# Low parts of weights made by an accumulating DMA instead of a subtraction on VectorE

## The chip, the core and the metric

The kernel runs on one core of a Trainium2 chip. The core has five engines that run their own instruction queues in order and meet at semaphores: TensorE (PE, with its weight loads shown as PEld), VectorE (DVE), ScalarE (ACT), GpSimd (POOL) and SyncE (SP, which issues the kernel's DMAs). Sixteen DMA engines move the data. The metric is the time of one execution on the device in microseconds, as a median of several runs; lower is better.

## What is computed

One layer of a hybrid backbone, for 128 context tokens and 512 latent tokens of width 1024, which the kernel holds side by side as 640 columns:

```python
h = rmsnorm(x, norm1) * (1 + sc1) + sh1
p = h @ w_in
qkv, z, ab, glu, gates = jnp.split(p, SPLITS, axis=-1)
qkv = jax.nn.silu(dwconv_seq(qkv, conv_qkv))
...
o, s_fin = bidir_delta(q, k, v, g, beta, s0)      # 8 heads, chunked delta rule, both directions
y_a = (rmsnorm(o, norm_o) * silu(z)) @ w_a_out
y_b = silu(layernorm(dwconv(glu branch), ln_g, ln_b)) @ w_b_out
x = x + g1 * ((ga * y_a + gb * y_b) @ w_o)
gu = (rmsnorm(x, norm2) * (1 + sc2) + sh2) @ w_gu
x = x + g2 * ((silu(gu[..., :FF_DIM]) * gu[..., FF_DIM:]) @ w_down)
```

The weights and the activations are float32. The context's delta states are an output beside the two token blocks.

## The kernel before

**A product of two float32 matrices is made of three products.** Each operand is split into a high part (the value rounded to the type float32r, `wh`, `hh`) and a low part (what the rounding left, `wl`, `hl`). A projection adds `wh*hh`, `wh*hl` and `wl*hh` in PSUM. The helper `split` (lines 106 to 108) makes both parts: ACT writes the high part (line 107), and DVE or POOL subtracts it from the raw value (line 108).

**Weights.** `load_w` (line 117) brings a block of 128 columns of a weight matrix, 1024 rows in 8 tiles of 128, so 128 partitions x 1024 float32, 512 KB: SP issues the load into `wr` (line 121), then `split` writes `wh` and `wl`. A `wl` lies in the same bytes as its `wr`; there are 4 such slots (`NWR`) and 2 buffers for `wh` (`NWH`). During most of the input projection every second slot carries raw weights of the modulation matrix `w_ada` (line 458), so a projection's slot comes back every second projection. `low["eng"]` chooses who subtracts: DVE until the delta rule and the branches beside it have ended, POOL after that.

**Projections.** `proj` (line 131) goes over the `nk` tiles of a weight block (8, or 4 for the two branch outputs) and for each over the three products and two column halves of 256 and 384; the matmul is line 143. A full projection is 48 matmuls. 56 such projections make up `w_in`: 24 for q, k and v, 8 for z, 16 for the gates, 8 for the convolution branch. `w_a_out` (first half of its rows) and `w_b_out` add 8 each of 4 tiles before the switch of `low["eng"]`.

**Beside them** run the steps of the delta rule for four pairs of heads: short convolutions and a substitution on DVE (lines 478, 593 to 611), small matmuls on PE, evacuations of PSUM on ACT, masks, powers and casts on POOL (lines 516, 584, 598, 607, 623, 650). Generators yield estimated costs, and a scheduler that works on an estimated timeline sets each engine's order when the program is built, so a queue's order is fixed and an instruction that waits holds what stands behind it. After the switch come the output projection and the FFN.

Of the kernel before, what the change touches and what calls it, by code (L numbers as in the profile page):

```python
# [9 lines left out]
F32 = mybir.dt.float32  # L10
# [4 lines left out]
AF = mybir.ActivationFunctionType  # L15
ALU = mybir.AluOpType
# [3 lines left out]
P = 128  # L20
# [36 lines left out]
def hybrid_step(ctx, tc, I, O):  # L57
    nc = tc.nc
    es = ctx.enter_context
    V, S_, G, PE = nc.vector, nc.scalar, nc.gpsimd, nc.tensor  # L60
# [39 lines left out]
    def g3(ap, a):  # L100
        return ap.rearrange("p (a b) -> p a b", a=a)
# [4 lines left out]
    def split(hi, lo, x, lo_eng=None):  # L106
        S_.activation(hi, x, AF.Identity)  # L107
        return (lo_eng or V).tensor_tensor(out=lo, in0=x, in1=hi.bitcast(F32), op=ALU.subtract)  # L108
# [3 lines left out]
                          mybir.DependencyInfo(mybir.DependencyClass.NoSync, mybir.DependencyReason.DATA),  # L112
                          reason="order")

    low = {"eng": V}

    def load_w(src, lo_eng=None, after=None, wh=None):
        a, b = src.shape[1], src.shape[2]
        n = a * b
        wr, wl = next(w_next)  # L120
        ld = nc.sync.dma_start(out=g3(wr[:, :n], a), in_=src)
        if after is not None:
            order(ld, after)
        wh = T_("wh", "wh", F32R) if wh is None else wh
        split(wh[:, :n], wl[:, :n], wr[:, :n], lo_eng or low["eng"])
        return g3(wh[:, :n], a), g3(wl[:, :n], a)

    def cols_of(w, c0, n=P):
# [2 lines left out]
    def proj(w, xh, xl, nk, pp=None, hfs=(0, 1), cut=HALVES, tiled=False):  # L131
        pp = pp or mm_pair()
        wh, wl = w
        for kt in range(nk):
            for j, (a, b) in enumerate(((wh, xh), (wh, xl), (wl, xh))):
                for hf in hfs:
                    c = cut[hf]
                    out, x = pp[hf][:, :c.stop - c.start], b[kt // 4]
                    if tiled:
                        out, x = g3(out, (c.stop - c.start) // P), x[:, c.start // P:c.stop // P, kt % 4, :]  # L140
                    else:
                        x = x[:, kt % 4, c]
                    PE.matmul(out, a[:, kt, :], x,  # L143
                              start=(kt == 0 and j == 0), stop=(kt == nk - 1 and j == 2))
        return pp

    def halves(pp, ap, cut=HALVES):
# [21 lines left out]
    for k, (nm, n) in enumerate((("c_ctx", 8), ("c", 8), ("norm1", 8), ("norm2", 8))):  # L169
        src = I[nm] if nm == "c_ctx" else I[nm][0]  # L170
# [89 lines left out]
    for pr in range(4):  # L260
# [7 lines left out]
        for kk in range(NK):  # L268
            for g in range(4):
                j, k = g // 2, g % 2  # L270
                PE.matmul(pa[32 * g:32 * g + 32, :P], sc[:, kk, 14:46], ws[j][:, kk, 128 * k:128 * k + 128],
                          start=(kk == 0), stop=(kk == NK - 1), tile_position=(0, 32 * g))
# [4 lines left out]
        for k in range(2):  # L277
            kt = 2 * pr + k
# [1009 lines left out]
```

## Time and profile before

| what | us |
|---|---|
| median of 3 runs (1337.16 to 1340.9) | 1338.35 |
| profiled execution, whole | 1341.02 |
| its span, first to last instruction | 1339.2 |
| PE busy | 1278.0 (95%) |
| DVE busy | 845.0 (63%) |
| ACT busy | 505.2 (38%) |
| POOL busy | 299.7 (22%) |

A profile shows for every engine when each instruction ran, which line and tiles it belongs to, and what ended the idle time before it. Busy shares over the whole span hide that the stages differ: DVE is at nine tenths or more in many slices of the first 800 us and at a quarter after. Matmuls overlap in the pipeline, so PE can be called busy and still not run at full pace; how fast a projection goes is better read from the starts of its matmuls.

### The profile page before, as it was taken

What the parts mean: (1) busy time and instruction counts of PE and PEld (TensorE: products, weight loads), DVE (VectorE), ACT (ScalarE), POOL (GpSimd) and SP (SyncE); (2) the same over time, 40 slices, a digit from 0 to 9 for tenths busy, and PEclk for the clock granted to TensorE, in tenths of its full rate; (3) what the DMA queues carried; (4) which work ended last, traced back from release to release, by engine and by line L of the source; (5) the groups of instructions that cost most, each with busy time, mean ns of one, the idle gap of its engine ahead of it and who ended that gap; (6) DMA issues with size and microseconds to landing.
All of it is one profiled execution on the core that took longest, in us unless ns stands there. A gap on an engine that the chain in (4) does not pass through costs nothing.

```text
span 1339.2 us, 23242 instructions
## 1 busy us (share of the span) xinstructions
PE 1278.0 (95%) x9180; PEld 1203.7 (90%) x9180; DVE 845.0 (63%) x1663; ACT 505.2 (38%) x1080; POOL 299.7 (22%) x306
## 2 busy tenths in 40 slices
PE   4998998997999999999998999999999999999997
PEld 4998997997998999999988998899988999889996
DVE  5788996989667899998687774621224212243136
ACT  3426646254354554525354323422221222112223
POOL 2103312220110312211010036433300333003304
PEclk8998999999999999999999999999999999999999
DMA  9523353343343453324456882122222222222222
GB/s 290 153 64 97 113 167 123 112 139 99 109 122 102 142 144 101 105 78 128 142 188 202 286 281 87 52 76 79 79 74 70 78 80 75 68 79 79 79 68 91
DMA packets 180333, 157.31 MB, mean 117 GB/s; under 512 B 9072, under 2 KB 151809, under 8 KB 180225
## 3 DMA queue, kind: packets, MB, share of 16 engines
q1 hardware_dynamic: 180225, 155.83, 37.6%
q8 instruction: 72, 1.18, 0.4%
q14 instruction: 36, 0.29, 0.1%
HBM read 131.80 MB, written 24.00 MB: 116 GB/s over the span
## 4 chain that ended last, share of the span: by engine, by line
PE 57%; DVE 8%; DMA 3%; issue 2%; ACT 2%; POOL 1%; SPq 0%; POOLq 0%; DVEq 0%; ACTq 0%
PE mm L143 36%; PE sm L1108 9%; PE mm L1108 4%; PE sm L143 1%; DVE wl L108 1%; PE sm L729 1%; DVE uacc L843 1%; PE sm L753 1%; PE sm L656 1%; DVE uacc L840 1%; PE sm L1153 1%; PE sm L716 1%; PE sm L709 1%; PE sm L739 1%; DMA wr<-in_w_in 1%
## 5 line engine op out<-in xcount | busy, mean ns | idle before, releaser
L107 ACT ACTIVATE wh<-wr 128x1024 fp32r<-128x1024 f32 (+1 forms) x154 | 152.6, 992 | 477.2 <-PE mm L143 186.1
L143 PE MATMUL mm<-hh,wh 128*128 128x256 f32 (+1 forms) x896 | 217.6, 318 | 0.9 <-ACT wh L107 0.9
L143 PE MATMUL mm<-hl,wh 128*128 128x256 f32 (+1 forms) x896 | 215.4, 314 | 0.0
L108 POOL TENSOR_TENSOR wl<-wr,wh 128x1024 fp32r<-128x1024 f32 (+1 forms) x59 | 133.2, 2259 | 356.7 <-ACT wh L107 337.2
L143 PE MATMUL mm<-hh,wl 128*128 128x256 f32 (+1 forms) x896 | 212.5, 314 | 0.0
L108 DVE TENSOR_TENSOR wl<-wr,wh 128x1024 fp32r<-128x1024 f32 (+1 forms) x95 | 109.7, 1155 | 105.7 <-ACT wh L107 94.4
L143 PEld LDWEIGHTS mm<-hh,wh 128*128 128x128 f32 x896 | 161.5, 190 | 6.8 <-issue 4.6
L143 PEld LDWEIGHTS mm<-hl,wh 128*128 128x128 f32 x896 | 164.5, 189 | 0.0
L143 PEld LDWEIGHTS mm<-hh,wl 128*128 128x128 f32 x896 | 162.7, 189 | 0.3 <-issue 0.2
L143 PE MATMUL mm<-h2h,wh 128*128 128x256 f32 (+1 forms) x672 | 155.7, 309 | 0.0
L143 PE MATMUL mm<-h2l,wh 128*128 128x256 f32 (+1 forms) x672 | 154.9, 308 | 0.0
L143 PE MATMUL mm<-h2h,wl 128*128 128x256 f32 (+1 forms) x672 | 154.6, 307 | 0.0
L1254 DVE TENSOR_TENSOR ft<-ft,mm 128x256 f32<-128x256 f32 (+1 forms) x42 | 18.6, 481 | 189.9 <-PE mm L143 189.8
L143 PEld LDWEIGHTS mm<-h2l,wh 128*128 128x128 f32 x672 | 123.1, 188 | 0.0
L143 PEld LDWEIGHTS mm<-h2h,wl 128*128 128x128 f32 x672 | 122.7, 188 | 0.0
L143 PEld LDWEIGHTS mm<-h2h,wh 128*128 128x128 f32 x672 | 122.0, 188 | 0.2
L478 DVE SCALAR_TENSOR_TENSOR acc<-ci,colA,acc 128x642 f32<-128x642 f32 x96 | 85.8, 894 | 7.6 <-ACT acc L476 7.1
L1108 PE MATMUL sm<-wh,fl 128*128 128x512 f32 x152 | 60.0, 395 | 0.0
L1108 PE MATMUL sm<-wh,fh 128*128 128x512 f32 x152 | 59.8, 393 | 0.0
L1108 PE MATMUL sm<-wl,fh 128*128 128x512 f32 x152 | 59.6, 392 | 0.0
L108 DVE TENSOR_TENSOR fl<-ft,fh 128x640 fp32r<-128x640 f32 x22 | 46.5, 2112 | 16.5 <-ACT fh L107 16.5
L604 DVE TENSOR_TENSOR stmp<-M,X 128x30 f32<-128x30 f32 (+14 forms) x120 | 44.6, 372 | 2.6 <-POOL X L598 1.0
(347 smaller groups left out, 2446.8 us busy)
## 6 DMA issues: line engine op xcount, KB each, us to landing
wr<-in_w_in SPq DMA_DIRECT2D x56, 512.0 KB
wr<-in_w_gu SPq DMA_DIRECT2D x44, 512.0 KB
wr<-in_w_ada SPq DMA_DIRECT2D x32, 512.0 KB
wr<-in_w_down SPq DMA_DIRECT2D x22, 512.0 KB
wada<-in_w_ada SPq DMA_DIRECT2D x8, 1024.0 KB
atd<-et SPq DMA_DIRECT2D x40, 128.0 KB
aux<-atd SPq DMA_DIRECT2D x40, 128.0 KB
tgd<-tgt SPq DMA_DIRECT2D x16, 320.0 KB
```

The source lines that it names most:

```text
L107: S_.activation(hi, x, AF.Identity)
L108: return (lo_eng or V).tensor_tensor(out=lo, in0=x, in1=hi.bitcast(F32), op=ALU.subtract)
L143: PE.matmul(out, a[:, kt, :], x, start=(kt == 0 and j == 0), stop=(kt == nk - 1 and j == 2))
L478: V.scalar_tensor_tensor(out=acc[:, :n], in0=ci[:, k:k + n], scalar=vA[:, k, ct:ct + 1], in1=acc[:, :n], op0=ALU.mult, op1=ALU.add)
L604: V.tensor_tensor(out=t, in0=bc(M[:, j + 1:, j:j + 1], [P, n, j]), in1=bc(X[:, j:j + 1, 0:j], [P, n, j]), op=ALU.mult)
L656: PE.matmul(pt[:, j, :], lhs[j], rhs[j], start=True, stop=True)
L709: PE.matmul(pr[:, d, j, :], TT[j].kT[:, ck[d], :], S[:, d, j, :], start=True, stop=True)
L716: PE.matmul(pq[:, d, j, :], TT[j].q2[:, OFFC[ck[d]]:OFFC[ck[d]] + P], S[:, d, j, :], start=True, stop=True)
L729: PE.matmul(pv[:, d, j, :], Y1[:, d, j, ck[d], :], rhs, start=True, stop=True)
L739: PE.matmul(pS[:, d, j, :], TT[j].ktok[:, ck[d], :], vw[:, d, j, :], start=True, stop=True)
L1108: PE.matmul(acc[i], a[kt // 4][:, kt % 4, c], b[:, k2, :], start=(kt == 0 and j == 0), stop=(kt == nk - 1 and j == 2))
L1254: V.tensor_tensor(out=d, in0=d, in1=s, op=ALU.mult)
```

## The change

While `low["eng"]` is `None`, which it is from the start until the delta rule and the branches end, `load_w` no longer subtracts. ACT writes `wh` from the raw weights as before, then ACT writes minus `wh` into `wl`, over the raw weights, and then POOL issues a DMA that reads the same weights from memory a second time and adds them onto `wl`. After the switch `split` works on POOL as before; calls that name an engine keep it. The second edit is in `proj`, for all projections: all products with `wh` come first, over all weight tiles, and all products with `wl` come after them.

```diff
-    low = {"eng": V}
+    low = {"eng": None}
...
-        split(wh[:, :n], wl[:, :n], wr[:, :n], lo_eng or low["eng"])
+        if lo_eng is None and low["eng"] is None:
+
+            S_.activation(wh[:, :n], wr[:, :n], AF.Identity)
+            S_.activation(wl[:, :n], wh[:, :n].bitcast(F32), AF.Identity, scale=-1.0)
+            G.dma_start(out=g3(wl[:, :n], a), in_=src, accum_op=ALU.add)
+        else:
+            split(wh[:, :n], wl[:, :n], wr[:, :n], lo_eng or low["eng"])
...
-        for kt in range(nk):
-            for j, (a, b) in enumerate(((wh, xh), (wh, xl), (wl, xh))):
-                for hf in hfs:
-                    c = cut[hf]
...
+        three = ((wh, xh), (wh, xl), (wl, xh))
+
+        for kt, j in [(kt, j) for kt in range(nk) for j in range(2)] + [(kt, 2) for kt in range(nk)]:
+            a, b = three[j]
+            for hf in hfs:
+                c = cut[hf]
```

The built program has 72 accumulating DMAs (56 of `w_in`, 8 of `w_a_out`, 8 of `w_b_out`), 72 more activations on ACT and 72 fewer subtractions on DVE. The changed code is 8 lines longer, so a line of before stands 8 higher there.

On PE, in the first projections of heads, the three products alternated with each weight tile. Before, at the fourth and fifth tile of one projection (the suffixes 132 and 133 are the two halves of the activations' rows):

```order
L143 MATMUL mm<-hh_132,wh 128x256
L143 MATMUL mm<-hh_132,wh 128x384
L143 MATMUL mm<-hl_134,wh 128x256
L143 MATMUL mm<-hl_134,wh 128x384
L143 MATMUL mm<-hh_132,wl_60 128x256
L143 MATMUL mm<-hh_132,wl_60 128x384
L143 MATMUL mm<-hh_133,wh 128x256
L143 MATMUL mm<-hh_133,wh 128x384
```

And in the change, at the end of the high weights of such a projection:

```order
L151 MATMUL mm<-hh_133,wh 128x256
L151 MATMUL mm<-hh_133,wh 128x384
L151 MATMUL mm<-hl_135,wh 128x256
L151 MATMUL mm<-hl_135,wh 128x384
L151 MATMUL mm<-hh_132,wl_58 128x256
L151 MATMUL mm<-hh_132,wl_58 128x384
```

The first matmul that reads `wl` is now the 33rd of 48; it was the 5th.

On POOL, around the end of the first pair's substitution (X, and its casts into XB) and the start of the second pair's masks, before:

```order
L584 AFFINE_SELECT Bt<-Bt 128x640 x2
L607 MEMSET X 128x32
L623 CAST XB<-T_1579 32x10x32 x4
L623 CAST XB<-T_1580 32x10x32 x4
L589 MEMSET Cc 128x384
L598 AFFINE_SELECT X<-M 128x1024
L650 TENSOR_TENSOR L_671<-Bt,off_102 128x512
```

And in the change (wl_56 and wl_60 are the low parts in two of the four slots):

```order
L129 DMA wl_56<-in_w_in 128x8x128
L592 AFFINE_SELECT Bt<-Bt 128x640 x2
L615 MEMSET X 128x32
L631 CAST XB<-T_1587 32x10x32 x4
L631 CAST XB<-T_1588 32x10x32 x4
L597 MEMSET Cc 128x384
L129 DMA wl_60<-in_w_in 128x8x128
L129 DMA wl_56<-in_w_in 128x8x128
L606 AFFINE_SELECT X<-M 128x1024
L129 DMA wl_60<-in_w_in 128x8x128
```

The DMAs stand between steps that wait for DVE: the masks, the memset of X and the casts all do. Of the 72 DMAs, 33 have at least one such step (a mask, a power, a memset of X, a cast or an off-diagonal product) between themselves and the DMA ahead.

## Rows read from the trace of the kernel before

**Rows 1.** Busy time of each engine by stage; PEclk is the granted clock.
```profile
core 0: us, PE busy (x) PEld busy (x) DVE busy (x) ACT busy (x) POOL busy (x), PEclk, DMA share, GB/s
0.00:100.00 100.00, 81.30 (x718) 77.61 (x719) 74.29 (x174) 35.49 (x67) 14.66 (x50) 0.93 0.56 170
100.00:500.00 400.00, 376.21 (x3145) 350.93 (x3143) 330.39 (x689) 207.59 (x550) 84.02 (x133) 0.98 0.40 123
500.00:650.00 150.00, 148.40 (x1161) 145.09 (x1160) 142.28 (x336) 65.65 (x121) 28.41 (x28) 1.00 0.36 105
650.00:800.00 150.00, 140.49 (x1045) 137.36 (x1044) 108.89 (x227) 56.10 (x132) 18.05 (x15) 0.98 0.70 226
800.00:1339.00 539.00, 531.62 (x3121) 492.73 (x3119) 189.13 (x239) 140.32 (x210) 154.60 (x80) 0.99 0.25 77
```

**Rows 2.** PE's longest waits, 100 to 500 us: total, times, longest.
```profile
PE sm L656 <- ACT XA L621: 4.6, 2, 2.3
PE sm L489 <- DVE K L523: 4.3, 1, 4.3
PE sm L739 <- DVE vw L735: 4.2, 2, 2.5
PE sm L709 <- ACT Sn L742: 2.1, 1, 2.1
```

**Rows 3.** Splits on DVE, 100 to 500 us: busy, mean ns | idle before.
```profile
L108 DVE TENSOR_TENSOR wl<-wr,wh 128x1024 fp32r<-128x1024 f32 x32 | 40.2, 1256 | 18.6 <-ACT wh L107 18.3
```

**Rows 4.** DVE and ACT, lines 108 and 107, 0 to 770 us.
```profile
L108 DVE TENSOR_TENSOR wl<-wr,wh 128x1024 fp32r<-128x1024 f32 (+1 forms) x72 | 81.5, 1133 | 32.2 <-ACT wh L107 31.7
...
L107 ACT ACTIVATE wh<-wr 128x1024 fp32r<-128x1024 f32 (+1 forms) x73 | 70.0, 959 | 130.9 <-PE mm L143 74.6 <-DMA wr<-in_w_in 50.9 <-DMA wr<-in_w_b_out 3.9
```

**Rows 5.** Two weight loads, issue and first reader: start, us, engine.
```profile
121.91 0.42 SPq L121 DMA_DIRECT2D wr<-in_w_in  x1
...
126.12 1.06 ACT L107 ACTIVATE wh<-wr 128x1024 fp32r<-128x1024 f32 x1 [0.68 <-DMA wr<-in_w_in]
...
17.32 3.61 SPq L121 DMA_DIRECT2D wr<-in_w_in  x1
...
28.64 1.06 ACT L107 ACTIVATE wh<-wr 128x1024 fp32r<-128x1024 f32 x1 [11.75 <-DMA wr<-in_w_in]
```

**Rows 6.** A piece of the chain that ended last: start, us, what.
```profile
353.83 7.57 DMA wr<-in_w_in
```

**Rows 7.** A tight projection: ACT timeline; PE matmuls, first and last start.
```profile
455.99 1.06 ACT L107 ACTIVATE wh<-wr 128x1024 fp32r<-128x1024 f32 x1 [0.19 <-DMA wr<-in_w_in]
...
L143 PE MATMUL mm<-hh,wh x16: 278/336/384, 458.6 to 464.9; 128*128 128x256 f32 x8, 128*128 128x384 f32 x8
...
L143 PE MATMUL mm<-hh,wl x16: 279/336/367, 459.2 to 466.6; 128*128 128x256 f32 x8, 128*128 128x384 f32 x8
```

**Rows 8.** A loose projection, the same three views.
```profile
524.90 1.06 ACT L107 ACTIVATE wh<-wr 128x1024 fp32r<-128x1024 f32 x1 [5.33 <-PE mm L143]
...
L143 PE MATMUL mm<-hh,wh x16: 278/336/365, 533.1 to 542.5; 128*128 128x256 f32 x8, 128*128 128x384 f32 x8
...
L143 PE MATMUL mm<-hh,wl x18: 279/331/364, 532.8 to 544.0; 128*128 128x256 f32 x9, 128*128 128x384 f32 x9
```

**Rows 9.** SP timeline: two successive loads into one weight slot.
```profile
439.94 0.37 SPq L121 DMA_DIRECT2D wr<-in_w_in  x1
...
458.11 0.38 SPq L121 DMA_DIRECT2D wr<-in_w_in  x1
```

**Rows 10.** POOL's waits for DVE, 100 to 500 us: total, times, longest.
```profile
POOL rn L516 <- DVE rn L515: 88.5, 14, 12.9
POOL Bt L584 <- DVE Bt L578: 63.2, 6, 15.9
...
POOL X L607 <- DVE X L606: 20.4, 2, 16.6
...
POOL XB L623 <- DVE T L610: 16.0, 2, 9.8
```

**Rows 11.** The start: a wait of PE, and the DVE timeline.
```profile
PE mm L143 <- ACT hh L288: 2.4, 1, 2.4
...
29.73 1.23 DVE L108 TENSOR_TENSOR wl<-wr,wh 128x1024 fp32r<-128x1024 f32 x1 [1.78 <-ACT wh L107]
```

More of the change, by code (lines that the diff above doesn't have):

```diff
@@ L133, in proj @@
         wh, wl = w
-        for kt in range(nk):
-            for j, (a, b) in enumerate(((wh, xh), (wh, xl), (wl, xh))):
-                for hf in hfs:
-                    c = cut[hf]
[L138 to L144, printed above, removed]
+        three = ((wh, xh), (wh, xl), (wl, xh))
[3 more added lines that the diff above has]
+                c = cut[hf]
+                out, x = pp[hf][:, :c.stop - c.start], b[kt // 4]
+                if tiled:
+                    out, x = g3(out, (c.stop - c.start) // P), x[:, c.start // P:c.stop // P, kt % 4, :]
+                else:
+                    x = x[:, kt % 4, c]
+                PE.matmul(out, a[:, kt, :], x,
+                          start=(kt == 0 and j == 0), stop=(kt == nk - 1 and j == 2))
         return pp
```

## The prediction

> **What bounds the kernel now.** I read the stages first, then who holds PE up, then how a weight block travels. By stage [rows 1], PE stands for 18.7 of the first 100 us, for 23.8 of the 400 us from 100 to 500, for 1.6 of the next 150, for 9.5 from 650 to 800 and for 7.4 after. The change's new path ends with the delta rule, near 770 us, so it can win at most the 23.8 + 1.6 + 9.5 = 34.9 us between 100 and 800, and something of the start. In the same stages DVE is busy 330.4 of 400 and 142.3 of 150 us: it is the second bound, and in the third stage both are full. The waits of PE between 100 and 500 us name DVE and ACT about equally [rows 2]: 8.5 us in the two longest for DVE, 6.7 in the two longest for ACT. No wait of PE for a low part is among them: the order is such that weights are mostly there.
>
> How a block travels: SP issues the load, and the first reader starts 4.2 us later when nothing else is in the way [rows 5]; at the start of the kernel it is 11.3 us, with SP's issue alone 3.6 [rows 5], and on the chain of waits one load takes 7.6 us [rows 6]. Then ACT makes the high part in 1.06 us and DVE the low part in 1.26 us on average [rows 3], after which the block's matmuls can start.
>
> **The change part by part.**
>
> *Off DVE.* 72 subtractions go, 81.5 us of work, and the 32.2 us for which DVE stood before them, mostly for ACT's high part [rows 4]. Between 100 and 500 us it is 40.2 + 18.6 = 58.8 of 400 us [rows 3]. What of it PE gets back is bounded by 0 (in the stage from 500 to 650 us PE stands 1.6 us, so nothing is there to win) and by the 33.3 us that PE stands in the two stages where it does stand. DVE's work in the first of them falls by an eighth, its occupied time by a seventh. I take 12 us: half of the standing from 100 to 500, since DVE is named in about half of it and most of what DVE does late there is late behind something in its own queue.
>
> *Onto ACT.* 72 negations. One is an activation of the same size as the high part's, so 0.96 us in the mean [rows 4], 69 us in all, some 32 x 1.06 = 34 us of them between 100 and 500, where ACT is busy 207.6 of 400. Behind them in ACT's order stand the evacuations that PE waits for. Bounds: 0, as ACT has room, and the 6.7 us of its two longest waits once more [rows 2]. I take 2.
>
> *The wait for the low part.* It now lands late and is needed late. The high part is ready as before. From the start of ACT's high part to the landing of the low part pass 1.06 + 1.06 us on ACT, POOL's issue, and the transfer. The trace has no DMA issued by POOL and none that accumulates. POOL's issue I bound by SP's, 0.4 to 3.6 us [rows 5]; from there to the landing by the plain loads of the same bytes, 4.2 to 11.3 us less that issue [rows 5], with one of 7.6 us between [rows 6]. An accumulating transfer reads its destination too, so I take half as much again as the undisturbed load, 6.3 us, issue included, which is nearest to the 4.2 and the 7.6. Then the low part is there 2.1 + 6.3 = 8.4 us after ACT began. It is needed at two thirds of the projection. In a loose place that is at 533.1 + 2/3 x 10.9 = 540.4, 15.5 us after ACT began [rows 8], and even 11.3 us would do (13.4). In a tight place, where ACT began as the load landed, it is at 458.6 + 2/3 x 8.0 = 463.9, 7.9 us after [rows 7], so 0.5 us are missing; at 7.6 it would be 1.8, at 11.3 it would be 5.5. Tight places are those between about 425 and 505 us and a few between 195 and 335; going through the starts of the matmuls I count five projections of 54 that would miss, by 0.5 to 2.3 us. Taken: 3 us. Bounds: 0 at 4.2 us, and at 11.3 us some 30.
>
> A DMA issued by GpSimd is priced by the Trainium skill, page "DMA: Bandwidth & Descriptors", section "Anatomy of one DMA — SWDGE (gpsimd) path", at about 2.0 us plus the bytes over 436 KB per us, an estimate of 3.2 us for 512 KB; no run here shows it. By that price no low part would be late, and the sum would end 3 us lower.
>
> *Order of the products.* It costs PE nothing by itself: 48 matmuls and 48 weight loads either way. It frees the high part's buffer after two thirds of a projection, where ACT now stands 74.6 us for PE [rows 4]. This helps the term above; I count it at nothing. After 800 us it changes no more: PE is busy 531.6 of 539 us there [rows 1], and the low parts from POOL were not waited for.
>
> *DMA traffic.* 56 blocks of 512 KB and 16 of 256 KB are read a second time, 33.6 MB. Between 100 and 650 us the DMA engines are busy 0.36 to 0.40 [rows 1] and have room. From 650 to 800 us they are at 0.70 and move 226 GB/s x 150 us = 33.9 MB; 16 x 0.26 = 4.2 MB come on top, an eighth. Bounds 0 to 5 us (half of PE's 9.5 us of standing again); I take 1.
>
> *The start.* ACT's first negation goes ahead of the activations for `hh`, for which PE stands 2.4 us, and DVE's first subtraction of 1.23 us, which stood ahead of the modulation, goes [rows 11]: 1.06 against 1.23, nothing. Ahead of the first use of a low part PE has 80 matmuls of the first two projections, 13 us at the 48 in 8.0 us of [rows 7], so even a crowded 11.3 us about hides.
>
> *Sum.* -12 + 2 + 3 + 1 = -6 us on the profiled execution's 1341.0, so 1335; that execution is 2.7 us over the median, so **1332** for the median.
>
> **The rivals.**
>
> *POOL's queue holds the DMAs (slower).* POOL works in order, and between its DMAs stand steps that wait for DVE: between 100 and 500 us POOL stood 88.5 us for DVE before the powers, up to 12.9 at once, 63.2 before the masks, up to 15.9, 20.4 before the memsets of X, up to 16.6, and 16.0 before the casts, up to 9.8 [rows 10]. Before, nobody was behind them in a hurry. Now 33 of the 72 DMAs stand behind one. The whole of such a wait is no loss, because the scheduler put the DMA where it expects it; but where DVE comes later than expected by more than the spare time (15.5 - 8.4 = 7 us in a loose place, none in a tight one), PE stands, and with it everything queued on PE. With 6 such places at 3.5 us over the spare time it is 21 us on top: 1353. For it speaks that DVE's longest waits are as long as a projection; against it that DVE is relieved in the same stage.
>
> *The accumulating transfer takes 12 us or more (slower).* A slot holds two successive projections' blocks 18.2 us apart in the tight stretch [rows 9]. With the change a slot's round is load 4.2, two activations 2.1, DMA 12, last third of the matmuls 2.7: 21 us. That is 1.4 us more a projection over eight projections, 11 us, and the misses of the other tight and middling places, about 15 projections at 2 to 3 us: 38 in all, and the relief of 12 with it is lost as DVE waits for PE: about 1385. Decides from about 9 us on.
>
> *DVE starves POOL's DMAs (slower).* If a DMA issued by POOL went forward only while DVE is idle, it would have 7.7 us of 150 from 500 to 650 [rows 1] for 13 DMAs; 1 us needed for each would stretch that stage by some 100 us, to about 1440. Nothing in the trace shows it: POOL's own steps are done there, 28.4 us of them [rows 1]. The Trainium skill has this rule: the page "SBUF — State Buffer", section "SBUF: two separate sides", says that a DMA issued from GpSimd has its descriptors written by GpSimd, and that VectorE, in modes that take both of its port pairs, locks GpSimd out meanwhile. It would speak against this change, which puts such DMAs beside the fullest VectorE.
>
> *The relief does not reach PE (no change).* The DMAs hide and DVE has room, but PE's standing in the delta rule is the latency of chains from engine to engine, and the new order is no better: -12 becomes about -4, the sum +2, so 1338 +- 4.
>
> **How the numbers follow.** A measurement of this kernel can tell some 0.3%, 4 us, from no change. My forecast has 0.46 (own range 1320 to 1338; 0.42 of it faster, 0.04 within the bound). The relief that does not reach PE has 0.16 (0.13 within, 0.03 slower). POOL's queue has 0.20 (0.19 slower, 0.01 within), the long transfer 0.14 and starvation 0.04, all slower. So faster 0.42, same 0.18, slower 0.40. The range: below, the relief at twice what I took and no late low part, 1332 - 12 - 4 = 1316; above, the long transfer's 1385, beyond which half of it and starvation lie, about 0.11; below 1316 lie some 0.06.
>
> **What would show it.** Right: DVE's busy time from 100 to 500 us falls by about 40 us and ACT's rises by about 34; the accumulating DMAs land 5 to 8 us after POOL issues them; PE's waits for `wl` stay under 5 us in all, and PE's standing there falls to about 12 us. Wrong: waits of PE for the accumulating DMA of more than 10 us (then see whether POOL issued late, behind DVE, or the transfer was long); POOL's DMA instructions of several us each; loads into `wr` that take clearly longer than 4.2 us; or DVE relieved and PE standing as before.

## The result

The change makes the kernel slower: 1370.88 us (1369.5 to 1372.24 in four runs) against 1339.62 us before, a ratio of 1.0234 with a 95% interval of 1.0211 to 1.0257. That is 31 us more, where 6 us less were forecast. The time lies in the range, the direction is the wrong one.

### The profile page after: what moved, and what is told of

The parts are those of the page before. It is cut to its first block, busy times and chain, and to the rows that moved or that the text cites. A ratio compares the mean times of both kernels' runs of the same rounds, so it can differ in the third digit from the quotient of the medians.

```text
span 1370.0 us, 23442 instructions
## 1 busy us (share of the span) xinstructions
PE 1287.6 (94%) x9180; PEld 1206.4 (88%) x9180; DVE 759.1 (55%) x1591; ACT 570.2 (42%) x1152; POOL 405.5 (30%) x378
## 3 DMA queue, kind: packets, MB, share of 16 engines
q0 software_dynamic: 66688, 33.56, 20.1%
## 4 chain that ended last, share of the span: by engine, by line
PE 64%; DMA 14%; DVE 12%; ACT 5%; issue 3%; SPq 1%; POOL 1%; POOLq 0%; ACTq 0%; DVEq 0%
PE mm L151 40%; PE sm L1116 9%; PE mm L1116 4%; DMA wr<-in_w_in 4%; DVE uacc L851 2%; DMA wada<-in_w_ada 2%; PE sm L664 2%; DMA atd<-et 2%; DVE uacc L848 1%; DMA wr<-in_w_b_out 1%; PE sm L151 1%; DMA wl<-in_w_in 1%; DVE X L614 1%; PE sm L497 1%; DVE stmp L612 1%
## 5 line engine op out<-in xcount | busy, mean ns | idle before, releaser
L151 PE MATMUL mm<-hl,wh 128*128 128x256 f32 (+1 forms) x896 | 212.1, 314 | 0.0
L151 PE MATMUL mm<-hh,wl 128*128 128x256 f32 (+1 forms) x896 | 154.8, 319 | 14.6 <-issue 6.3
L129 POOL DMA_DIRECT2D wl<-in_w_in x56 | 88.2, 1575 | 257.2 <-ACT wl L128 131.9
L151 PEld LDWEIGHTS mm<-hh,wl 128*128 128x128 f32 x896 | 139.0, 192 | 16.3 <-issue 6.8
L151 PE MATMUL mm<-h2h,wl 128*128 128x256 f32 (+1 forms) x672 | 105.1, 308 | 0.0
L151 PEld LDWEIGHTS mm<-h2h,wl 128*128 128x128 f32 x672 | 101.1, 188 | 0.0
L108 DVE TENSOR_TENSOR wl<-wr,wh 128x1024 fp32r<-128x1024 f32 x23 | 28.2, 1224 | 90.3 <-ACT wh L107 90.3
L128 ACT ACTIVATE wl<-wh 128x1024 fp32r<-128x1024 f32 (+1 forms) x72 | 69.4, 963 | 1.4
```

Source lines behind the costliest of these rows:

```text
L128: S_.activation(wl[:, :n], wh[:, :n].bitcast(F32), AF.Identity, scale=-1.0)
L129: G.dma_start(out=g3(wl[:, :n], a), in_=src, accum_op=ALU.add)
L151: PE.matmul(out, a[:, kt, :], x, start=(kt == 0 and j == 0), stop=(kt == nk - 1 and j == 2))
```

## The profile after

Busy time by stage, to be read beside [rows 1] (PE, PEld, DVE, ACT, POOL, then the granted clock, the share of the DMA engines' time that is busy, and GB/s):

```profile
0.00:100.00 100.00, 73.85 (x665) 69.50 (x666) 66.00 (x165) 43.22 (x75) 26.15 (x57) 0.91 0.85 201
100.00:500.00 400.00, 374.74 (x3077) 346.30 (x3077) 293.26 (x637) 223.75 (x546) 127.17 (x160) 0.98 0.71 157
500.00:650.00 150.00, 143.57 (x1123) 138.11 (x1122) 127.53 (x301) 85.24 (x161) 54.26 (x48) 0.99 0.83 159
650.00:800.00 150.00, 134.73 (x1008) 131.17 (x1008) 91.38 (x223) 66.34 (x149) 32.21 (x26) 0.94 0.86 218
```

DVE is relieved: 293.3 us busy from 100 to 500 us, against 330.4. PE is not better off: it stands 25.3 of those 400 us, against 23.8, and 6.4 instead of 1.6 and 15.3 instead of 9.5 in the next two stages. What has grown most is the DMA engines' share: 0.40 to 0.71, 0.36 to 0.83, 0.70 to 0.86.

From the page of the changed kernel, the two large DMA queues (packets, MB, share of 16 engines' span; q0 carries the accumulating DMAs, q1 those that SP issues) and the accumulating DMAs of w_in (number, size, median us from issue to landing):

```profile
q1 hardware_dynamic: 180225, 155.83, 36.9%
q0 software_dynamic: 66688, 33.56, 20.1%
...
wl<-in_w_in POOLq DMA_DIRECT2D x56, 512.0 KB, 7.2
```

One packet of q0 took 0.201 x 16 x 1370 us / 66688 = 66 ns. What POOL paid to issue such a DMA (ns, minimum, median, maximum):

```profile
L129 POOL DMA_DIRECT2D wl<-in_w_in x56: 1532/1564/1758, 31.3 to 674.3; - x56
```

And where PE stands ahead of low weights. Behind the first bar stand busy us and mean ns, behind the second PE's idle time just before such matmuls, and what ended it. It was 0.0 us in the kernel before:

```profile
L143 PE MATMUL mm<-hh,wl 128*128 128x256 f32 (+1 forms) x896 | 212.5, 314 | 0.0
```

And in the change:

```profile
L151 PE MATMUL mm<-hh,wl 128*128 128x256 f32 (+1 forms) x896 | 154.8, 319 | 14.6 <-issue 6.3 <-DMA wl<-in_w_in 5.4 <-ACT acc L484 2.8
L151 PE MATMUL mm<-oh,wl 128*128 128x384 f32 (+1 forms) x128 | 23.0, 316 | 4.0 <-DMA wl<-in_w_a_out 4.0
```

That is 18.6 us. A piece of the chain of waits from the tight stretch (start, us, what) shows how it happens:

```profile
438.37 6.68 DMA wl<-in_w_in
445.09 2.64 PE mm L151 x16
...
448.33 5.53 PE mm L151 x36
453.87 3.66 DMA wr<-in_w_in
457.62 1.06 ACT wh L127
...
460.73 5.16 issue
465.89 2.15 PE mm L151 x7
...
511.02 9.02 DMA wl<-in_w_in
520.08 3.99 PE mm L151 x15
```

The 5.16 us called "issue" are also a wait for a low part: POOL issued that DMA at 454.4 us, it landed 11.4 us later, at 465.8, and the first matmul with low weights started at 465.9. This is the kind of row where the view names no releaser and the landing, read from the DMA's own entry, tells it.

## The experiments

All times are medians; ratios are against runs of the kernel before on the same chip (1336.9 to 1339.6 us), with 95% intervals. Diffs are against the changed kernel if nothing else is said. For each kernel "PE ahead of low weights" is the sum of the idle times in the rows of the kind shown above. In `e7_plain`, `e14_delay`, `e15_nodma`, `e16_half`, `e18_lag` and the two `e20` kernels the low parts hold other values than they should; that the time does not hang on the values is taken for granted, no run shows it.

### The two edits apart, and POOL instead of the DMA

`e1_order` is the kernel before with only the second edit.

> The kernel before with only the second edit: products with the high weights first, those with the low weights last; DVE subtracts as before. Theory (the 31 us come from the accumulating transfer: it takes 7.2 us in the median where a tight projection has room for less, and crowds the start): the order costs nothing by itself, the time is that of before, 1336 to 1342 us, and PE's standing from 100 to 500 us stays at 24 us. Rival (the order of the products, or what the scheduler makes of it, loses the time): most of the 31 us appear here, 1355 us or more.

Measured: 1351.87 us, ratio 1.0109 (1.0091 to 1.0127). Both expectations fail: the order alone costs 13 us, less than half of the 31 but far from nothing. Up to the last projection of w_in it costs nothing (that one ends 2.7 us earlier than before). In PE's order, though, 3053 matmuls of projections stand ahead of the delta rule's last scan step, where it was 2987 before: the scheduler made something else of the branch-output stage. The matmuls that transpose the last heads' output tell when the delta rule ends (duration in ns, then first and last start); before

```profile
L788 PE MATMUL sm<-ident,oacc x10: 272/272/273, 764.2 to 765.2; 128*128 128x128 f32 x10
```

and with the order alone

```profile
L790 PE MATMUL sm<-ident,oacc x10: 272/273/327, 779.4 to 780.7; 128*128 128x128 f32 x10
```

15 us later, and the last products of the branch output wait for them. In the changed kernel 2977 stand ahead of that step, so this loss is not in its 31 us.

`e12_order8` puts only projections of 8 weight tiles in the new order:

```diff
-        for kt, j in [...]:
+        late = [(kt, j) for kt in range(nk) for j in range(2)] + [(kt, 2) for kt in range(nk)]
+        for kt, j in late if nk == NK else [(kt, j) for kt in range(nk) for j in range(3)]:
```

> The kernel before with DVE subtracting, and the low-last order only in the projections of 8 weight tiles; the branch outputs (4 tiles) keep the interleaved order. The order alone cost 13 us, all of it after the last projection of w_in: in its built program 3053 matmuls of projections stand ahead of the delta rule's last scan step on PE, against 2987 before, so the delta rule's end, on which the output of the last heads waits, comes later. In this kernel it is 3025. Theory (the scheduler's placement of the scan among the projections costs the time, 66 matmuls too many cost 13 us): 38 too many cost 7 to 8 us, 1344 to 1348 us. Rival (the low-last order is itself slower in the branch outputs, with their 24 matmuls): 1336 to 1341 us, since they are interleaved here.

Measured: 1343.06 us, 1.0038 (1.0025 to 1.0050). 38 matmuls too many cost some 5 us, 66 cost 13: as far as two kernels can show it, the order's loss goes with the scan's place. It is less than in proportion, and the measured value lies between the two expected bands.

`e2_early` is the changed kernel with the products interleaved as before.

> The changed kernel with the three products interleaved as before, so that the low part is needed at the 5th matmul of a projection and not at the 33rd, some 4 to 6 us earlier. Theory: each projection from the 1st to the 42nd that now has less than 5 us to spare stands for the difference, about 25 of them by 3 to 5 us, so 1440 to 1490 us. Rival (the order loses the time): about 1340 us. Rival (ACT's negations or the second read's traffic lose it, lateness of the low part does not): 1365 to 1375 us.

Measured: 1431.21 us, 1.0695 (1.0672 to 1.0717); PE ahead of low weights 61.2 us in w_in alone, of which 40.0 are put down to the DMA. The low-last order does what it was made for: without it the accumulating DMA costs 60 us more. The 1440 expected was a little too much.

`e3_pool` is the kernel before in the new order, with POOL subtracting (`low = {"eng": G}`).

> The kernel before with the low-last order and POOL subtracting from the start instead of DVE: no second read, no accumulating transfer, no negation on ACT, but the subtraction stands in POOL's queue among the same steps that wait for DVE. A subtraction on POOL takes 2.4 us, so the low part is there about 5 us earlier than with the transfer. Theory: no late low parts, the relief of DVE shows what it is worth: 1325 to 1342 us. Rival (POOL's in-order queue holds the low parts behind steps that wait for DVE): 1355 us or more, with waits of PE for POOL's low part.

Measured: 1393.22 us, 1.0407 (1.0378 to 1.0435). Slower by 55 us, but not by the rival's mechanism: PE does not wait for POOL's low parts (0.0 us ahead of low weights), it waits for DVE. From 500 to 650 us PE stands 26.0 us, and 19.7 of them are put down to DVE. The stage from 500 to 650 us, here and with the order alone (columns as above):

```profile
500.00:650.00 150.00, 124.03 (x920) 117.40 (x920) 144.25 (x262) 63.73 (x132) 64.61 (x48) 0.94 0.34 93
```

```profile
500.00:650.00 150.00, 147.10 (x1142) 144.30 (x1141) 143.69 (x328) 66.06 (x121) 25.91 (x29) 1.00 0.38 105
```

DVE is as full as with its subtractions, and does 262 instructions instead of 328, of which 16 were subtractions. The reason is in the last section.

### The accumulation alone, and the ceiling

`e7_plain` takes `accum_op=ALU.add` from the DMA and nothing else. Every engine has the same instructions in the same order as in the change.

> The changed kernel with the accumulation taken out of POOL's DMA, which then writes the raw weights over the low part: the low part is replaced by the raw weights, everything else is as in the change. The same negations, the same bytes read twice, the same instructions on POOL. Theory (it is the accumulation that makes the transfer long: its packets of 512 bytes take some 66 ns of engine time against 27 ns of plain ones): POOL's transfers land 4 to 5.5 us after issue, the time falls to 1338 to 1350 us. Rival (the second read, POOL's issue or ACT's negation loses the time, whatever the DMA does with the bytes): 1362 to 1372 us.

Measured: 1344.63 us, 1.0044 (1.0024 to 1.0064). As the theory had it, and **26 of the 31 us are the accumulation's**. Its queue, its landing and its issue:

```profile
q0 software_dynamic: 66688, 33.56, 14.8%
...
wl<-in_w_in POOLq DMA_DIRECT2D x56, 512.0 KB, 5.3
```

```profile
L129 POOL DMA_DIRECT2D wl<-in_w_in x56: 876/889/1122, 31.5 to 653.7; - x56
```

The same packets take 0.148 x 16 x 1341.9 / 66688 = 48 ns instead of 66, the DMAs land after 5.3 us instead of 7.2, and POOL issues one in 0.89 us instead of 1.56. PE ahead of low weights:

```profile
L151 PE MATMUL mm<-hh,wl 128*128 128x256 f32 (+1 forms) x896 | 152.3, 315 | 4.7 <-issue 2.3 <-ACT acc L484 1.9 <-DMA wl<-in_w_in 0.5
L151 PE MATMUL mm<-oh,wl 128*128 128x384 f32 (+1 forms) x128 | 23.1, 318 | 2.3 <-DMA wl<-in_w_a_out 2.3
```

7.0 us, 11.6 less than in the change. Since the orders are the same, the starts of the projections can be laid side by side. The change falls back by 1.2 us at the start, by 5.7 more until the 13th projection, by another 4 at the 30th and by 10 from the 31st to the 40th; from the 40th to the 55th by nothing; and by 8 from there to the last branch output. 10 of the 21 us until the 40th appear exactly where a projection's first low weights are read (the 12th, 16th, 32nd, 34th and 39th). In the stretch where the loss is largest, from 436 to 472 us, four DMAs for low parts were issued, in the change and with plain transfers (minimum, median, maximum):

```profile
DMA to landing us min/median/max: 6.7/8.4/11.4
```

```profile
DMA to landing us min/median/max: 4.5/5.2/7.7
```

`e15_nodma` leaves POOL's DMAs out altogether.

> The changed kernel without POOL's DMAs: the low part is minus the high part and the second read is left out. It shows what the relief of DVE and the new order give with ACT's negations paid and nothing to wait for, so the ceiling of the change. My forecast's terms without those of the transfer (-12 of relief, +2 of ACT's) give 1328 us. Theory (the relief is worth the 7 us by which PE stood less between 100 and 500 us with the plain transfer, the start's 4 us are the transfers'): 1328 to 1336 us. Rival (the relief does not reach PE at all): 1337 to 1342 us.

Measured: 1324.95 us, 0.9899 (0.9870 to 0.9929), 12 us faster than before, 46 faster than the change and better than either expectation. The relief of DVE is real. PE's standing from 100 to 500 us (columns as above; the first line without DMAs, the second with plain ones):

```profile
100.00:500.00 400.00, 390.91 (x3231) 362.73 (x3231) 309.33 (x681) 239.77 (x578) 85.92 (x137) 1.00 0.42 125
```

```profile
100.00:500.00 400.00, 383.37 (x3190) 356.06 (x3188) 305.61 (x666) 234.42 (x580) 114.33 (x166) 0.99 0.65 166
```

9.1 us without the DMAs, 16.6 with plain ones, 25.3 with accumulating ones, 23.8 before.

### Where it is lost

`e4_start` subtracts the first two blocks on DVE (`... and len(blocks) > 2`).

> The changed kernel with the first two weight blocks subtracted by DVE, so that no accumulating DMA runs beside the loads of the start. PE's instruction order is that of the change. Theory: the 7 us that the third projection starts late go, but part of them was regained by the 30th projection anyway (there the change is 2.5 us behind): 1363 to 1370 us. Rival (the start's delay runs through to the end): 1361 to 1364 us. Rival (the start's delay is not the accumulating DMA's): 1369 to 1373 us.

Measured: 1368.45 us, 1.0228 (1.0202 to 1.0254); by its interval the time cannot be told from the change's. In the trace the third projection starts 2.9 us earlier, not 7: 4.5 us of its delay are not the accumulating DMA's, and with the order alone (`e1_order`) it is 3.5 us late already. Of the 2.9 us, 1.4 are left at the 55th projection, so the start is a minor part.

`e17_tail` gives the branch outputs back to DVE (the new branch only where `a == NK`).

> The changed kernel with the 16 weight blocks of the branch outputs (256 KB each, some time between 680 and 800 us) split by DVE as before, and the accumulating DMA for the 56 blocks of w_in alone. Against the plain transfers the change lost 8 us there and 21 us before. Theory: the 8 us come back and the 21 stay, 1360 to 1365 us. Rival (the branch outputs only inherit a delay from before): 1368 to 1373 us.

Measured: 1360.89 us, 1.0151 (1.0119 to 1.0183). The branch outputs' part comes back, 10 us, and the rest stays.

`e8_late` uses the accumulating DMA from the 40th block on (`... and len(blocks) > 39`).

> The changed kernel with the accumulating DMA only from the 40th weight block on; the first 39 are subtracted by DVE. All else, the low-last order too, as in the change. The scan's last step stands behind 2973 matmuls of projections, as in the change (2977) and about as before (2987). Theory (the loss lies where the low part is needed soonest, the start and the projections up to about the 42nd, and part of it in the branch outputs; the loose projections from the 43rd on hide the accumulating transfer): 1338 to 1346 us. Rival (the accumulating DMAs cost about the same anywhere, by their share of the engines' time): 33 of 72 of the 26 us, 1350 to 1356 us.

Measured: 1348.16 us, 1.0072 (1.0054 to 1.0091), between the two. PE ahead of low weights is 0.0 in w_in and 4.8 in the branch outputs: among the loose projections no low part is waited for, in the branch outputs some are. The loose projections are not free for that: the 42nd starts 1.3 us earlier than in the kernel before, the 56th 5.3 us later, and why is not shown.

`e13_sel` uses it for blocks 3 to 11, 20 to 31 and from 41 on.

> Accumulating DMAs only for the 3rd to 11th, the 20th to 31st and from the 41st weight block on, where the low parts landed mostly in time in the change; DVE subtracts the rest; the low-last order throughout. 2997 matmuls of projections stand ahead of the scan's last step, 10 more than before. Theory (a late low part costs only where the projection is tight): 1340 to 1350 us, most of what is lost being in the branch outputs, as with the DMAs from the 40th block on (1348 us). A version that beats the kernel before would be under 1334 us.

Measured: 1359.66 us, 1.0164 (1.0139 to 1.0190). The expectation was 10 us too low. Up to the last projection of w_in it is 3.5 us behind the kernel before, and then it loses 13 in the branch outputs, with PE ahead of low weights for 7.6 us there. That the same 16 blocks cost 6 us after the one and 13 after the other is not explained by what I can show.

`e10_ada` keeps the raw modulation weights out of the slots from the 29th to the 44th projection, and `e11_ada_before` does the same to the kernel before:

```diff
-        if ada_todo and len(units) > ADA_FROM:
+        if ada_todo and len(units) > ADA_FROM and not 28 < len(units) <= 44:
```

> The changed kernel with the raw blocks of the modulation weights kept out of the slots from the 29th to the 44th projection (they come beside the 45th to 56th instead), so that projections there have all four slots, load earlier, and the low part has twice the round to land in. Theory (the low parts are late in the tight stretch because the slot's round has no room for a transfer of 7 us): the late low parts of the 31st to 38th projection, 14 us together, go, the time falls to 1345 to 1360 us. Rival (the DMA engines' share is the limit, the bytes and packets being the same): 1366 to 1374 us.

> The kernel before with the raw blocks of the modulation weights moved from the 29th to 44th projection to the 45th to 56th, the control for the same move in the changed kernel, which gained 27 us up to the 42nd projection and gave 20 of them back between the 44th and the 54th. Theory (in the changed kernel the moved blocks collide with the accumulating transfers there; here nothing is late at either place): 1335 to 1343 us. Rival (the move costs its 20 us by itself, because the slots go short beside the 45th to 56th projection): 1350 us or more.

Measured: 1364.44 us, 1.0187 (1.0165 to 1.0210), and 1345.79 us, 1.0063 (1.0041 to 1.0086). The move gains 6 us in the change and loses 9 in the kernel before. Neither time lies in one of its bands. Up to the 43rd projection the change gains 27 us, and of the 14 us by which low parts of the 32nd to 39th landed after the last high matmul 5 are left; from the 45th to the 55th it gives 20 back, where the moved blocks now stand. The control gains 13 up to the 45th, 7 of them by the 43rd, and gives 15 back: the move costs by itself, though less than its rival had it. So some 20 of the 27 us are the change's own: with four slots for the projections the low parts of the tight stretch are hardly late, and the slots are then short elsewhere.

### Lateness, or the time on the DMA engines

The accumulation does two things: the low part is later, and the DMA engines are busy longer. These runs were to tell which one costs: theory A says the lateness, theory B the time on the DMA engines.

`e14_delay` puts `G.memset(wl[:, :n].bitcast(F32), 0.0)` ahead of the plain DMA. `e18_lag` puts four such memsets ahead of a plain DMA of a quarter of the block, `e20_lag2` and `e20_lag3` two and three. `e16_half` accumulates over half of the weight tiles (`[:, :a // 2]` on both sides of the DMA).

> The changed kernel with the accumulation taken out of POOL's DMA (so the low part is replaced by the raw weights) and, ahead of each such DMA, a memset of the same tile on POOL, about 1 us, which only delays it. The plain transfer alone gave 1344.6 us and landed 5.5 us after POOL issued it, the accumulating one 7.2 us; here the low part lands 6.5 to 7 us after POOL takes it up, while the DMA engines carry the plain transfers. Theory A (the lateness of the low part is what costs, whatever makes it late): more than half of the 26 us comes back, 1357 to 1368 us. Theory B (what costs is the time that accumulating packets take of the DMA engines, which slows the loads of the raw weights too): 1344 to 1352 us.

> The changed kernel with the accumulating DMA over only the first half of the weight tiles of each block; the second half of the low part stays minus the high part. Half the packets, all of the kind that takes 66 ns, so some 10% of the engines' span where the full plain transfers took 14.8% (1344.6 us) and the full accumulating ones 20.1% (1370.9 us). Theory B (the accumulating packets' time on the DMA engines costs, through all transfers that share them): less than with the plain transfers, 1330 to 1343 us, although the low part lands about as late as theirs (5.5 us) or later. Theory A (lateness of the low part, or accumulation by itself, costs): if it lands after 6 us or more, as the 256 KB ones of the change did (6.3 to 7.4 us), 1352 to 1368 us.

> Lateness with hardly any traffic: instead of the accumulating DMA four memsets of the low part on POOL (0.86 us each, 3.4 us) and then a plain DMA of a quarter of the block (128 KB); the low part is replaced by zeros and a quarter of raw weights. It is ready 7 to 9 us after ACT's negation, as in the change (8 to 13 us in the tight stretch), at a quarter of the plain transfers' engine time, but with 2.5 to 3 us more of POOL's time for each block. Theory B (engine time costs, lateness of this size hardly): 1328 to 1345 us. Theory A (lateness costs): 1355 to 1375 us. A loss could here also come from POOL's own queue; then PE waits for POOL's masks and casts, and not for the low part.

> As the kernel with four memsets and a plain DMA of a quarter block, with two memsets (1.7 us): that one was at 1367 us with low parts ready 9.9 us after ACT's negation in the median and up to 28 us, more than in the change (9.1, up to 15), and its scan stood elsewhere in PE's order (2852 matmuls ahead of its last step; here 2972, in the change 2977). Here the low part is ready some 7.5 us after the negation, as with the plain transfers (7.1), at a quarter of their bytes. Theory A (lateness costs): about as the plain transfers, 1338 to 1345 us. Theory B (engine time costs): nearer to the kernel without the DMAs (1325 us), 1326 to 1334 us.

> The same with three memsets (2.6 us): the low part is ready some 8.5 to 9 us after the negation, about as late as in the change (9.1), with a quarter of the bytes, all plain; 2971 matmuls ahead of the scan's last step. Theory A: 1355 to 1371 us. Theory B: 1328 to 1342 us. In between, both share the loss.

`e23_plan` is the change with `G.tensor_copy(wl[:, :n // 4], wl[:, :n // 4].bitcast(F32))` ahead of the accumulating DMA.

> The changed kernel with one more step between ACT's negation and the accumulating DMA: POOL copies a quarter of the low part onto itself (256 columns, under 1 us; no value changes). The transfers are the same, each a little later. But the scheduler knows of the copy: in the built program 524 matmuls run while one projection waits at its low weights and another has begun, against 149 in the change, and 2973 stand ahead of the scan's last step (2977 in the change). Theory C (what costs is lateness for which the order has no other work; PE stood 18.5 us straight ahead of low weights in the change and 70 us in all): although every low part is later, PE stands less ahead of them and the time falls, 1350 to 1364 us. Theory A (lateness as such): 1374 to 1385 us. Theory B (the engine time of the transfers, however the order is): 1366 to 1374 us.

Measured, sorted by time; "ready" is the median from the start of ACT's negation to the landing of the low part over the 56 blocks of w_in, and q0 the share of the DMA engines' span in POOL's transfers:

| kernel | us | ratio, 95% interval | q0 | ready, us | PE ahead of low weights, us |
|---|---|---|---|---|---|
| e15_nodma | 1324.95 | 0.987 to 0.993 | none | | 0.0 |
| e20_lag2 | 1335.12 | 0.995 to 0.999 | 3.7% | 7.3 | 2.0 |
| e20_lag3 | 1338.58 | 0.998 to 1.001 | 3.7% | 8.5 | 4.0 |
| e14_delay | 1339.68 | 1.000 to 1.003 | 14.3% | 8.0 | 8.3 |
| e16_half | 1340.13 | 1.000 to 1.003 | 10.7% | 6.9 | 7.6 |
| e7_plain | 1344.63 | 1.002 to 1.006 | 14.8% | 7.0 | 7.0 |
| e17_tail | 1360.89 | 1.012 to 1.018 | 17.8% | 9.2 | 16.0 |
| e23_plan | 1366.39 | 1.016 to 1.023 | 20.1% | 9.8 | 15.3 |
| e18_lag | 1367.31 | 1.018 to 1.026 | 3.6% | 9.9 | 2.1 |
| the change | 1370.88 | 1.021 to 1.026 | 20.1% | 9.1 | 18.6 |

By their bands: `e14_delay` came out below both, `e16_half` and `e20_lag3` in B's, `e20_lag2` 1 us above B's and 3 below A's, `e18_lag` in A's. Neither theory takes all of it. Against lateness as such: with three memsets the low part is ready only half a microsecond earlier than in the change and the time is 32 us less. Against that reading stands a thing that the first expectation left out: the scheduler knows of a memset and plans for it. By the traces, 139 matmuls run in the change between the last high and the first low matmul of the projections of w_in; with one memset it is 382, with three 877. The scheduler does not know that a DMA accumulates (the order is the same with and without), so what the accumulation adds is lateness without anything put in its place. That was theory C, and `e23_plan` was to show it: with 477 such matmuls (its expectation counts them in another way) its low parts are later than in the change, yet PE stands 15.3 us ahead of them instead of 18.6, and the time falls by 4.5 us. The two intervals overlap, and the time lies at the lower edge of what theory B gave: at best a small part. That the longer issue on POOL's own queue is the cost has little for it: with three memsets POOL is busy 528 us, in the change 405, and the former is the faster. `e16_half` landed after 5.2 us in the median, so the condition that should have told A from B did not come about; it shows only that half of the accumulating packets cost as little as all of the plain ones. `e18_lag` stands apart: PE hardly stands ahead of low weights, POOL is busy 586 us instead of 405, and only 2852 matmuls stand ahead of the last scan step, so its loss must come from elsewhere, and from where is not shown.

What is shown: with the same order, the accumulation costs 26 us. Of the 28 us between the two profiled spans (1370.0 and 1341.9), 11.6 are PE standing straight ahead of low weights, 6.8 are PE being busy longer with the same instructions (1287.6 against 1280.8 us, with the granted clock at 0.94 instead of 0.97 between 650 and 800 us), and the other 10 are standing at other places. By the waits of PE in the two traces these are spread: 4.3 more behind ACT's `et`, a tile of the delta rule, 3.1 more ahead of the transposes that end the last heads' output, 2.8 more for the modulation's weights (`wada`) in the first 100 us, 2.1 more for `vw` on DVE, and smaller ones of either sign. What stays open is what makes each of these late, and whether they would go if all lateness were planned for.

## Why the prediction was wrong

**Off DVE, -12.** Right in what reaches PE: without the DMAs the kernel gains 12.0 us, and PE's standing there falls from 23.8 to 9.1 us, where about 12 were said. The rival that the relief does not reach PE falls with this. In the busy time, DVE is down by 37 us between 100 and 500, where about 40 were said, but part of that is work that comes later in the change: without the DMAs it is 21 us less, since DVE then gets more of its other work done there. Over the whole span it is 85.9 us less, for 81.5 us of subtractions.

**Onto ACT, +2.** Busy 16 us more between 100 and 500 us, where 34 were said, since the change is behind in its work by 500 us; without the DMAs it is 32. The 12 us gained include this cost, so relief and negations together are -12 where -10 was forecast.

**The wait for the low part, +3: this step failed.** Against plain transfers in the same order the accumulation costs 26 us. The transfer's length was taken as 6.3 us with bounds of 4.2 to 11.3, and it is 7.2 in the median; I said it would land 5 to 8 us after issue, and most did. What failed is the count of what is missed. Five projections by 0.5 to 2.3 us were to stand; by the trace nine low parts of w_in land after the last high matmul has begun, by up to 5.7 us, and PE stands 18.6 us ahead of low weights in all. Two things were left out. I counted with one length everywhere, although the transfer takes 6.4 us in the median from 300 to 430 us and 8.4, at most 11.4, from 436 to 472 us, where weights are tight. Raw weights, a modulation block and the accumulating transfer run beside each other there; that this makes it long is likely, but not shown alone. SP's issues around the one of 454.4 us:

```profile
447.76 0.37 SPq L121 DMA_DIRECT2D wr<-in_w_in  x1
448.42 1.29 SPq L466 DMA_DIRECT2D wr<-in_w_ada  x1
453.87 0.37 SPq L121 DMA_DIRECT2D wr<-in_w_in  x1
455.62 0.34 SPq L466 DMA_DIRECT2D wr<-in_w_ada  x1
```

And I took ACT's negation as following the high part at once, 1.1 us after its start; in the 12th, 17th and 32nd projection it began 3.3, 3.9 and 2.3 us after. The bound of "some 30 us at 11.3 us" was in the working, and the term was put at the low end of it. The prediction's own sign of being wrong, more than 10 us of such waits, came about.

**DMA traffic, +1: this step failed too.** With bounds of 0 to 5 it was reckoned from bytes alone and for one stage. Plain transfers of the same bytes put the kernel 20 us behind the one without any (1344.6 against 1325.0), their own late low parts of 7.0 us and POOL's issue of 0.89 us each included. `e20_lag2`, with a quarter of the bytes and low parts ready about as late, is 10 us behind the one without and 10 ahead of the plain ones, so about half of the 20 may be the traffic's, if its memsets change nothing else. I read 0.36 to 0.40 of the engines' time as room; a plain second read brings it to 0.65 and 0.70, the accumulating one to 0.71 and 0.83.

**Order of the products, 0.** Right for the change only by luck: there the scan stands behind 2977 matmuls of projections, before behind 2987. Alone the same edit moved it by 66 and cost 13 us. The built order shows this; the prediction went by two places of it and not by the scan's.

**The start, 0.** PE stood 26.2 us in the first 100 us against 18.7, and the third projection starts 7 us late: half of it the new order's, 3 us the accumulating DMAs', which run beside the modulation's loads. 5 of the 7 are regained by the 31st projection, and in the trace of `e4_start` 1.4 us are left of what the DMAs did there.

**The sum.** Without the DMAs -12.0 us, with plain transfers 19.7 more, with the accumulation 26.3 more: +34. That it is not the 31 measured lies in the kernel before, at 1336.9 us on one chip and at 1339.6 on the other.

**The rivals.** POOL's queue (1353): not it. Of the 56 DMAs of w_in POOL took up 49 within 1.6 us of the start of ACT's negation, the other seven within 5.4. The long transfer (1385, from about 9 us on) comes nearest: its mechanism, the slot's round that has no room in the tight stretch, is what was seen, at 7.2 us in the median and up to 11.4 in that stretch. From the 32nd to the 37th projection the load for the next block in a slot is issued 0.03 to 0.11 us after the last matmul with the slot's low weights, as at 447.73 and 447.76 us above. The rounds of the two slots from 447.8 and 453.9 us on take 22.8 and 24.5 us, and the same two with plain transfers 19.8 and 21.4. That its price of 1.4 us a projection over eight projections, 11 us, comes near the 10 us that the change lost against plain transfers between the 31st and the 40th is luck: it was reckoned for 12 us, and at 8.4 us the same sum gives a round of 17.4 us, which is under the 18.2 of before. The rest of that rival was added up short: 11 us and 15 times 2 to 3 us make 41 to 56, not 38, so by its own terms it stood at 1385 to 1400. DVE starving POOL's DMAs (1440): no; POOL issued every one of 512 KB in 1.53 to 1.76 us, also from 500 to 650 us, where DVE was busy 127.5 of 150. The Trainium skill's rule in "SBUF — State Buffer", section "SBUF: two separate sides", by which this could have happened, shows no trace here: these DVE operations did not hold up the issue. The Trainium skill's price for such a DMA, in "DMA: Bandwidth & Descriptors", section "Anatomy of one DMA — SWDGE (gpsimd) path", an estimate of 3.2 us for 512 KB, is far below the medians here, 5.3 us for the plain and 7.2 us for the accumulating one; the shortest plain one took 3.3.

No version that ran beats the kernel before and computes all of it. The gain to be had is the 12 us of DVE's relief; a way to make low parts elsewhere than on DVE must cost less than that in transfers, and neither POOL's arithmetic (1393) nor these DMAs do.

## What to carry to other kernels

Before moving work from an engine to a DMA, find the stretch where weights arrive just in time and price the transfer there, with the loads that run beside it, not by its median elsewhere; a mean share of 0.40 for the DMA engines was not room in this one. An accumulating DMA was dearer here than a plain one in POOL's issue (1.56 against 0.89 us), in engine time (66 against 48 ns a packet) and in landing (7.2 against 5.3 us), and a scheduler that does not know this leaves the wait uncovered. After an edit that only reorders, compare where every chain that ends late stands in the built order, not only the place that was edited.

## What the runs showed of the hardware

The same blocks in 66688 packets in all (33.56 MB, some 500 bytes each) took 48 ns a packet of engine time plain and 66 ns accumulating, and POOL's instruction for 512 KB 0.89 and 1.56 us. SP's packets of 512 bytes took 30 ns in the mean in the same trace as the 48, so a plain packet from POOL was dearer than one from SP too.

A two-input subtraction on POOL slowed DVE's operations beside it. With POOL subtracting, DVE was busy 837.7 us, with DVE itself making the same 72 subtractions it was 821.9. The convolution's multiply-adds on DVE, with DVE subtracting and with POOL subtracting (mean ns behind the bar):

```profile
L480 DVE SCALAR_TENSOR_TENSOR acc<-ci,colA,acc 128x642 f32<-128x642 f32 x96 | 87.3, 910 | 5.6 <-ACT acc L478 4.8
```

```profile
L480 DVE SCALAR_TENSOR_TENSOR acc<-ci,colA,acc 128x642 f32<-128x642 f32 x96 | 114.0, 1188 | 13.2 <-ACT acc L478 12.1
```

The additions of a matmul's result to `acc`, with one input in PSUM, kept their median: 281 ns in the one, 280 in the other. The Trainium skill's page "SBUF — State Buffer", section "SBUF: two separate sides", has a rule for it: a DVE operation with two SBUF inputs and a GpSimd operation that reads SBUF shut each other out for a whole instruction. The trace agrees: such a multiply-add takes 0.88 us in the median, and the longest went from 1.88 to 3.04 us, 2.2 over the median, where a subtraction on POOL takes 2.46 in the mean.
